# Hybrid decoder block on one core: a transpose of attention factors handed on one step later, one of two gather copies on ScalarE in the late steps, and two merge loads written in front of a loop's end

## The chip, the core and the metric

The kernel runs on one core of a Trainium2 chip. A core has TensorE (PE: matmuls, with PEld for its weight loads), VectorE (DVE), ScalarE (ACT), GpSimd (POOL) and SyncE (SP), which here issues nearly all transfers between the chip's memory and the core. Each engine works through its own instructions in the order in which they were written; engines wait for one another by semaphores. Results of matmuls go to eight banks of an accumulation memory, here two rings of four, named "mm" and "acc".

The metric is the device time of one execution in microseconds (us). The kernel before takes 1875.59 us, the median of three runs (1875.35 to 1877.91).

## The reference

One layer, 1024 tokens of width 1024, everything in float32:

```python
h = h + 0.5 * swiglu(rms_norm(h, ffn1_norm), ffn1_w1, ffn1_w3, ffn1_w2)
u = rms_norm(h, mix_norm)
proj = u @ w_in                     # q, k, v of 12 heads; 512 pooled channels; two gates
y_attn = dilated_mixture_attention(q, k, v) @ w_branch_attn
y_pool = multiscale_pool(pz, pool_w, pool_scale) @ w_branch_pool
merged = gates[:, :, 0] * y_attn + gates[:, :, 1] * y_pool
h = h + merged @ w_out
h = h + 0.5 * swiglu(rms_norm(h, ffn2_norm), ffn2_w1, ffn2_w3, ffn2_w2)
return rms_norm(h, final_norm)
```

The attention has three groups of four heads, each with its own window and dilation. Every group gives an output and a softmax denominator for each token; the three outputs of a head slot are added with weights that come from the three denominators. Those weights are called factors below.

## The kernel before

Every float32 factor of a product is split into a high and a low part, and a product is three matmuls: high by high, high by low, low by high. ACT makes the high part by a copy, DVE or POOL the low part by a subtraction. The large products are done in blocks, with sums and differences of blocks, so that seven products stand for eight.

The program goes through the first feed-forward net (0 to about 600 us), the input projection (to about 1020), the token mixers with the pooled branch (to about 1135), the merge and the output projection (to about 1236), and the second feed-forward net with the last norm.

**The first products.** `run_first(n, ks, terms)` (matmuls at line 1158) makes the first product of quad n over the blocks ks of the inner dimension. Term 0 is high by high, 1 is high by the low part of the input x, 2 is the low part of the weight by high. Quads 0 and 1 have a bank each (u_first); both need the low parts xlo_b_f of blocks 2 and 3, which DVE makes.

**The mixers.** Attention works on 48 slots: two pairs of heads (hp), three groups, eight blocks of queries. The loop takes two slots a step; q counts 24 steps. In step q, PE makes the scores s (for two steps at a time, when q is even), turns the exponentials of step q-1 (`trans_p`, tile tp), does pieces of the pooled branch's product (yp) as filling, and makes the outputs of step q-2 (`values`, tile o). ACT makes the high part of the turned exponentials (ehi), splits the next ring of queries and keys (line 1590), and takes the exponentials (e). DVE copies the outputs of step q-3 from their bank to their place by token (`gather`, two copies of 64 partitions by 256, line 2071), masks the scores and makes the low parts elo. `house(s)` does what falls due at a slot: statistics out and back, loads of values, and the next piece of the factors.

**The factors.** `make_factors(hp, eng)` is a generator; each `advance` runs it to its next `yield`. For head pair 0 it makes the factors f by small operations, turns them on PE (f_turned, line 1917, into an "mm" bank), copies them out by ACT (1919), stores them (f_by_head, 1920), and, a yield later, loads them spread over the partitions by four loads f_of (1928; two for the first half of the tokens, two for the second). For head pair 1 it spreads them by two copies of ACT and one of DVE (1937, 1935).

**Combining.** `combine(hp, half, ...)` multiplies the three outputs of a half of the tokens with their factors and adds them: for hp 0 on POOL (lines 2081 and 2085), then ACT makes the high part att (2090) and POOL the low one (2091). For hp 1, after the loop, PE turns the factors (fa), DVE multiplies (2083), and POOL and DVE add. Steps 20 to 23 take hp 0's pieces between the other work; the last piece of the second half follows after the loop, in front of the last pair's ehi on ACT.

**After the loop.** Eight pieces n of hp 1's combining alternate with the last of the 48 pieces of the pooled branch. `end_branches` multiplies a finished pooled product by its gate (line 2124), and `send` stores it (by_pool, 2134). `load_merge(k)` loads a gate and a pooled product (2161, 2162) for merge k. Then PE multiplies by the branch weights (ya), DVE and POOL merge, and the output projection wo (2368) begins with the merged sums' high and low parts (o_hi, o_lo).

Of the kernel before, what the change touches and what calls it, by code (L numbers as in the profile page):

```python
# [12 lines left out]
AF = mybir.ActivationFunctionType  # L13
# [124 lines left out]
def tile_block(  # L138
# [895 lines left out]
    def begin_up1():  # L1034
# [94 lines left out]
        banks = {}  # L1129
# [20 lines left out]
        def run_first(n, ks, terms):  # L1150
            if n not in banks:
                banks[n] = quads[n].bank["x"] = bank("mm", f"u_first{n}")
            w, (hi, lo) = first[n], X["b11"]
            for i in terms:
                for k in ks:
                    r = slice(k * P, (k + 1) * P)
                    a, b = three((w[:, 0, r], w[:, 1, r]), (hi[:, k, :], lo[:, k, :]))[i]
                    pe.matmul(banks[n], a, b, start=(k == 0 and i == 0), stop=(k == 3 and i == terms[-1]))

        FRONT, BACK = slice(0, 2 * P), slice(2 * P, HALF)  # L1160
        high("b11", 0, xt(0, 0), gain(0))
# [31 lines left out]
            high("b11", k, xt(0, k), gain(k))  # L1193
        for k in (2, 3):
            low("b11", k, xt(0, k), gain(k))
        run_first(0, (2, 3), (0, 2, 1))
        run_first(1, (2, 3), (0, 2, 1))
        operand(2, 1)
        operand(3, 1)
        high_b21(4)  # L1200
# [186 lines left out]
    class Mix:  # L1387
# [56 lines left out]
        def send(self):  # L1444
            for a in range(2):
                nc.sync.dma_start(gate_dram[self.g][:, a], self.y[a])
# [447 lines left out]
    def make_factors(hp, eng):  # L1894
# [19 lines left out]
        if hp == 0:  # L1914
            yield
            p = bank("mm", "f_turned")[:GROUPS * 2 * NT, :P]
            pe.transpose(p, by_head.rearrange("p g a i -> p (g a i)"), ident)
            turned = att_small.tile([GROUPS * 2 * NT, P], F32, name="f_turned")
            ac.activation(turned, p, AF.Copy)
            nc.sync.dma_start(f_dram.rearrange("g a i p -> (g a i) p"), turned)  # L1920
            yield
# [133 lines left out]
    def gather(q):  # L2055

        hp, g, i = slots[2 * q]
        del T[2 * q], T[2 * q + 1]
        p = outs.pop(q).rearrange("p (s a c) -> p s a c", s=2, a=2)
        if i == 0:  # L2060
            own[hp, g] = sums_o.tile([P, S], F32, tag="o", bufs=HPAIRS * GROUPS, name=f"o{hp}_{g}")
        o = own[hp, g]
        if g == 0:
            o = o[:, i * P:(i + 2) * P].rearrange("p (s c) -> p s c", s=2)
        elif g == 1:
            o = o.rearrange("p (b c r) -> p r b c", b=2, r=4)[:, i // 2]
        else:
            o = o.rearrange("p (c i) -> p i c", i=NT)[:, i:i + 2]
        for a in range(2):
            r = slice(a * HD, (a + 1) * HD)  # L2070
            ve.tensor_copy(o[r], p[r, :, a, :])

    att_parts = {}

# [115 lines left out]
    def house(s):  # L2190

        u, i = divmod(s, NT)
        if i == 1 and u > 0 and slots[s - 2][1] != 0:
            send_stats(*slots[s - 2][:2])
        if s - N // 2 in (8, 9, 10, 11, 12):
            advance(factors[0])
        if i == 4 and u + 1 < len(uses):
            load_values(uses[u + 1])
# [8 lines left out]
    with tc.manual_schedule():  # L2207
# [6 lines left out]
                    for hp, (adds, lower) in enumerate((((gp, gp), gp), ((gp, ve), ve)))]  # L2214
        splits = {}
        for q in range(N // 2):
            send()
            if q % 2 == 0:
                scores(q)
                scores(q + 1)  # L2220
            for half in {20: (0, 0), 21: (0,), 22: (0, 1), 23: (1, 1)}.get(q, ()):
                advance(combines[0][half])
            if q == 0 or q % 2 == 1:
                next(fill, None)
            if q > 0:
                trans_p(q - 1)
                splits[q - 1] = split_p(q - 1)
                next(fill, None)
                if q % 4 == 1:
                    next(fill, None)  # L2230
# [46 lines left out]
        for n in range(8):  # L2277
            advance(combines[1][n // 4])
            if n not in (3, 5, 7):
                next(fill, None)  # L2280
            end_branches()
            send()
            if n == 3:
                load_merge(2)
        for k in (3, 4):
            load_merge(k)
    assert next(fill, None) is None
    left_b.close()
    xstack.close()
# [398 lines left out]
```

## Time and profile before

| what | us |
|---|---|
| median of three runs | 1875.59 |
| the profiled execution | 1877.42 |
| its span, from the first to the last instruction | 1875.2 |
| PE busy | 1863.7 |
| DVE busy | 1366.2 |
| POOL busy | 783.9 |
| ACT busy | 768.4 |
| transfers, mean | 181 GB/s |

The granted clock of PE was 0.999 of full speed over the span. A row of the timeline gives the start and the length of one instruction, or of a few that follow one another on one engine, then engine, line, operation, out<-in, shapes, the count, and in brackets how long the engine sat idle before and what ended that. A row of groups gives total busy time and the mean length in ns. A row of stretches gives, for each engine, its busy us and instructions, then the granted clock, the share of the 16 transfer engines that were busy, and GB/s.

### The profile page before, as it was taken

What the parts mean: (1) busy time and instruction counts of PE and PEld (TensorE: products, weight loads), DVE (VectorE), ACT (ScalarE), POOL (GpSimd) and SP (SyncE); (2) the same over time, 40 slices, a digit from 0 to 9 for tenths busy, and PEclk for the clock granted to TensorE, in tenths of its full rate; (3) what the DMA queues carried; (4) which work ended last, traced back from release to release, by engine and by line L of the source; (5) the groups of instructions that cost most, each with busy time, mean ns of one, the idle gap of its engine ahead of it and who ended that gap; (6) DMA issues with size and microseconds to landing.
All of it is one profiled execution on the core that took longest, in us unless ns stands there. A gap on an engine that the chain in (4) does not pass through costs nothing.

```text
span 1875.2 us, 24419 instructions
## 1 busy us (share of the span) xinstructions
PE 1863.7 (99%) x8667; PEld 1545.1 (82%) x8667; DVE 1366.2 (73%) x1966; ACT 768.4 (41%) x1393; POOL 783.9 (42%) x569
## 2 busy tenths in 40 slices
PE   9999999999999999999999999999999999999998
PEld 8888888888888888888888887888888888888886
DVE  7887866668886776658885886887765566577867
ACT  7422323233345643334445772463333333343344
POOL 5554644452222364445554467544333333312221
PEclk9999999999999999999999999999999999999999
DMA  8134324356565436765578888634332233354654
GB/s 327 45 124 149 121 95 152 117 206 209 192 231 198 157 114 208 258 211 185 213 251 324 314 254 298 267 129 180 120 139 85 90 107 122 126 203 157 223 197 146
DMA packets 148369, 339.70 MB, mean 181 GB/s; under 512 B 18024, under 2 KB 39576, under 8 KB 146712
## 3 DMA queue, kind: packets, MB, share of 16 engines
q1 hardware_dynamic: 144504, 327.30, 50.1%
q10 hardware_dynamic: 3744, 10.85, 1.6%
q8 instruction: 68, 1.11, 0.2%
q14 instruction: 53, 0.43, 0.1%
HBM read 237.48 MB, written 100.62 MB: 180 GB/s over the span
## 4 chain that ended last, share of the span: by engine, by line
PE 55%; DVE 2%; ACT 2%; DMA 1%; issue 1%; POOL 1%; SPq 0%; ACTq 0%; POOLq 0%; DVEq 0%
PE u_mixm L334 15%; PE d_f L904 8%; PE wo L2368 4%; PE yp L2110 2%; PE o L2048 1%; PE u_f20a L334 1%; PE u_f20b L334 1%; PE u_f21b L334 1%; PE u_f21a L334 1%; PE u_f210b L334 1%; PE u_f210a L334 1%; PE u_f29b L334 1%; PE u_f29a L334 1%; PE u_f28b L334 1%; PE u_f28a L334 1%; PE u_f27b L334 1%
## 5 line engine op out<-in xcount | busy, mean ns | idle before, releaser
L904 PE MATMUL d_f<-bhi_f,ahi_f 128*128 128x512 f32 x616 | 240.2, 390 | 0.0
L904 PE MATMUL d_f<-bhi_f,alo_f 128*128 128x512 f32 x616 | 239.8, 389 | 0.0
L904 PE MATMUL d_f<-blo_f,ahi_f 128*128 128x512 f32 x616 | 239.7, 389 | 0.0
L861 POOL TENSOR_TENSOR alo_f<-g_f,ahi_f 128x512 fp32r<-128x512 f32 x60 | 86.7, 1462 | 269.0 <-ACT ahi_f L857 269.0
L334 PE MATMUL u_mixm<-xhi_t_mix,wc_mixm 128*128 128x512 f32 x608 | 157.3, 391 | 0.1
L904 PEld LDWEIGHTS d_f<-bhi_f,alo_f 128*128 128x128 f32 x616 | 115.6, 188 | 24.3 <-DVE alo_f L861 0.2
L904 PEld LDWEIGHTS d_f<-bhi_f,ahi_f 128*128 128x128 f32 x616 | 115.6, 188 | 24.1 <-ACT h L424 0.5
L904 PEld LDWEIGHTS d_f<-blo_f,ahi_f 128*128 128x128 f32 x616 | 115.7, 188 | 24.0
L334 PEld LDWEIGHTS u_mixm<-xhi_t_mix,wc_mixm 128*128 128x128 f32 x608 | 113.5, 188 | 23.8 <-ACT wc_mixm L322 0.5
L334 PE MATMUL u_mixm<-xhi_b_mix,wc_mixm 128*128 128x512 f32 x456 | 120.3, 391 | 0.0
L325 POOL TENSOR_TENSOR wc_mixm<-s_mixm,wc_mixm 128x512 fp32r<-128x512 f32 x52 | 77.1, 1483 | 101.8 <-ACT wc_mixm L322 95.7
L334 PEld LDWEIGHTS u_mixm<-xhi_b_mix,wc_mixm 128*128 128x128 f32 x456 | 84.9, 188 | 17.2
L322 ACT ACTIVATE wc_mixm<-s_mixm 128x512 fp32r<-128x512 f32 x76 | 47.0, 628 | 111.4 <-DVE s_mixm L378 56.4
L857 ACT ACTIVATE ahi_f<-g_f 128x1024 fp32r<-128x1024 f32 x84 | 81.9, 975 | 6.8 <-DMA g_f<-gs_f 6.6
L334 PE MATMUL u_mixm<-xlo_t_mix,wc_mixm 128*128 128x512 f32 x304 | 81.3, 389 | 0.0
L325 POOL TENSOR_TENSOR wc_mixm<-raw,wc_mixm 128x512 fp32r<-128x512 f32 x41 | 62.3, 1522 | 37.9 <-ACT wc_mixm L322 24.6
L2368 PE MATMUL wo<-w_o,o_hi 128*128 128x512 f32 x224 | 69.4, 391 | 0.0
L646 POOL TENSOR_TENSOR y_f<-y_f,norm_ffn 128x512 f32<-128x512 f32 x35 | 54.4, 1560 | 35.5 <-DVE y_f L627 25.2
L857 ACT ACTIVATE bhi_f<-s_f2w 128x512 fp32r<-128x512 f32 x55 | 32.9, 627 | 86.0 <-DVE s_f2w L879 69.6
L857 ACT ACTIVATE bhi_f<-s_f1w 128x512 fp32r<-128x512 f32 x55 | 33.1, 629 | 83.5 <-DVE s_f1w L879 70.8
L334 PEld LDWEIGHTS u_mixm<-xlo_t_mix,wc_mixm 128*128 128x128 f32 x304 | 57.1, 188 | 12.0
L861 DVE TENSOR_TENSOR alo_f<-g_f,ahi_f 128x1024 fp32r<-128x1024 f32 (+1 forms) x48 | 58.6, 1222 | 7.7 <-ACT ahi_f L857 7.7
(1360 smaller groups left out, 4823.4 us busy)
## 6 DMA issues: line engine op xcount, KB each, us to landing
g_f<-gs_f SPq DMA_DIRECT2D x70, 512.0 KB
gs_f<-y_f SPq DMA_DIRECT2D x88, 256.0 KB
raw<-in_w2a_dram SPq DMA_DIRECT2D x35, 512.0 KB
raw<-in_w2b_dram SPq DMA_DIRECT2D x35, 512.0 KB
gs_f<-gb_f SPq DMA_DIRECT2D x46, 256.0 KB
raw<-in_w1b_dram SPq DMA_DIRECT2D x22, 512.0 KB
raw<-in_w3b_dram SPq DMA_DIRECT2D x22, 512.0 KB
raw<-in_w1a_dram SPq DMA_DIRECT2D x20, 512.0 KB
```

The costliest lines, as they stand in the source:

```text
L322: ac.activation(w[:, 0], src, AF.Copy)
L325: eng.tensor_tensor(w[:, 1], src, w[:, 0].bitcast(F32), op=OP.subtract)
L334: pe.matmul(p, a, b, start=(start and n == 0), stop=(n == 11), skip_group_check=not start)
L646: gp.tensor_tensor(c, c, self.sv.norm[:, cols], op=OP.mult)
L857: ac.activation(hi[:, c], src, AF.Copy)
L861: eng.tensor_tensor(lo[:, d], src[:, o], hi[:, d].bitcast(F32), op=OP.subtract)
L904: pe.matmul(self.banks[m][t], l, r, start=(first and q == 0), stop=(last and q == 2))
L2048: pe.matmul(p, l, r, start=(j == 0), stop=(j == end))
L2110: pe.matmul(p, a, b, start=(j == 0), stop=(j == 11))
L2368: pe.matmul(banks[m][t], l, r, start=(st == 0 and j == 0 and q == 0), stop=(st == 1 and j == 1 and q == 2))
```

## The change

It has four parts. In the first products, the terms 0 and 2 of both quads over blocks 2 and 3 now come before term 1 of both. The turned factors get one more `yield`, and their pieces other places. From the gather of step 17 on, the second of the two copies goes from DVE to ACT; and the pieces of hp 0's combining in steps 22 and 23 change order. The loads of merges 3 and 4 are written into the loop after it.

```diff
@@ run_first
-                    pe.matmul(banks[n], a, b, start=(k == 0 and i == 0), stop=(k == 3 and i == terms[-1]))
+                    pe.matmul(banks[n], a, b, start=(k == 0 and i == 0), stop=(k == 3 and i == 1))
@@ the first products
-        run_first(0, (2, 3), (0, 2, 1))
-        run_first(1, (2, 3), (0, 2, 1))
+        for terms in ((0, 2), (1,)):
+            for n in (0, 1):
+                run_first(n, (2, 3), terms)
@@ make_factors
             pe.transpose(p, by_head.rearrange("p g a i -> p (g a i)"), ident)
+            yield
             turned = att_small.tile([GROUPS * 2 * NT, P], F32, name="f_turned")
             ac.activation(turned, p, AF.Copy)
             nc.sync.dma_start(f_dram.rearrange("g a i p -> (g a i) p"), turned)
@@ gather
         for a in range(2):
             r = slice(a * HD, (a + 1) * HD)
-            ve.tensor_copy(o[r], p[r, :, a, :])
+            if a == 1 and 3 * N // 8 - 1 <= q:
+                ac.activation(o[r], p[r, :, a, :], AF.Copy)
+            else:
+                ve.tensor_copy(o[r], p[r, :, a, :])
@@ house
-        if s - N // 2 in (8, 9, 10, 11, 12):
+        if s - N // 2 in (8, 9, 10, 12):
             advance(factors[0])
@@ the loop over q
         for q in range(N // 2):
+            if 2 * q == N // 2 + 14:
+                advance(factors[0])
             send()
...
-            for half in {20: (0, 0), 21: (0,), 22: (0, 1), 23: (1, 1)}.get(q, ()):
+            for half in {20: (0, 0), 21: (0,), 22: (1, 1), 23: (0, 1)}.get(q, ()):
                 advance(combines[0][half])
...
                 splits[q - 1] = split_p(q - 1)
+                if 2 * q == N // 2 + 12:
+                    advance(factors[0])
                 next(fill, None)
@@ after the loop
             send()
-            if n == 3:
-                load_merge(2)
-        for k in (3, 4):
-            load_merge(k)
+            if n in (3, 4, 5):
+                load_merge(n - 1)
```

N is 48, so the transpose of the factors goes from the end of step 17 to step 18, behind `trans_p`; its copy and store to the end of step 18, in front of that slot's loads of values and statistics; and the four loads f_of to the start of step 19.

On ACT, the copy of the turned factors stands here before. ehi is the high part of the turned exponentials of one step, xlo_b_mix<-xhi_b_mix the split of a ring, and e the exponentials of one slot:

```order
L1995 ACTIVATE e_9743,own_stats_2_9681<-e_9743,own_stats_2_9681 128x128 x2
L1995 ACTIVATE e_9746,own_stats_2_9681<-e_9746,own_stats_2_9681 128x128 x2
L1919 ACTIVATE f_turned<-f_turned 48x128
L2027 ACTIVATE ehi_9825<-tp_0_9801 128x512
L1590 ACTIVATE xlo_b_mix<-xhi_b_mix 128x512 x2
L1995 ACTIVATE e_9819,own_stats_2_9681<-e_9819,own_stats_2_9681 128x128 x2
L1995 ACTIVATE e_9822,own_stats_2_9681<-e_9822,own_stats_2_9681 128x128 x2
```

And now, at the same place:

```order
L1997 ACTIVATE e_9743,own_stats_2_9681<-e_9743,own_stats_2_9681 128x128 x2
L1997 ACTIVATE e_9746,own_stats_2_9681<-e_9746,own_stats_2_9681 128x128 x2
L2029 ACTIVATE ehi_9822<-tp_0_9796 128x512
L1591 ACTIVATE xlo_b_mix<-xhi_b_mix 128x512 x2
L1997 ACTIVATE e_9816,own_stats_2_9681<-e_9816,own_stats_2_9681 128x128 x2
L1997 ACTIVATE e_9819,own_stats_2_9681<-e_9819,own_stats_2_9681 128x128 x2
L1921 ACTIVATE f_turned<-f_turned 48x128
```

The copy has moved behind the whole of the next step.

On SP, the store and the loads of the factors stand here before, between loads for the pooled branch (gb, wab), values (v) and statistics (stats):

```order
L1627 DMA gb_9756<-gate_3625 128x1024
L1920 DMA f_by_head<-f_turned 48x128
L2134 DMA by_pool_8629<-gb_9247 128x1024
L1928 DMA f_of_9838<-f_by_head 64x3x512 x4
L1611 DMA v_0_in<-v_3612 128x1024
L1611 DMA v_1_in<-v_3612 128x1024
L1889 DMA stats_8617<-st_1_8622 128x8x4
L1622 DMA wab_9950<-late_w_105 128x2x512
```

And now:

```order
L1628 DMA gb_9756<-gate_3625 128x1024
L2139 DMA by_pool_8629<-gb_9247 128x1024
L1922 DMA f_by_head<-f_turned 48x128
L1612 DMA v_0_in<-v_3612 128x1024
L1612 DMA v_1_in<-v_3612 128x1024
L1890 DMA stats_8617<-st_1_8622 128x8x4
L1930 DMA f_of_9843<-f_by_head 64x3x512 x4
L1623 DMA wab_9950<-late_w_105 128x2x512
```

A pooled store has moved ahead of the factors' store, and two loads of values and one of statistics ahead of the four loads f_of.

Further on in SP's queue stand the merge loads of the loop's end, each a gate and a pooled product; by_pool_8632 is the last pooled store. Before:

```order
L2161 DMA merge_10277<-gate_3623 128x512
L2162 DMA merge_10277<-by_pool_8629 128x512
L2134 DMA by_pool_8632<-gb_9952 128x1024
L2161 DMA merge_10308<-gate_3625 128x512
L2162 DMA merge_10308<-by_pool_8631 128x512
L2161 DMA merge_10311<-gate_3620 128x512
L2162 DMA merge_10311<-by_pool_8626 128x512
```

And now:

```order
L2166 DMA merge_10277<-gate_3623 128x512
L2167 DMA merge_10277<-by_pool_8629 128x512
L2139 DMA by_pool_8632<-gb_9952 128x1024
L2166 DMA merge_10292<-gate_3625 128x512
L2167 DMA merge_10292<-by_pool_8631 128x512
L2166 DMA merge_10302<-gate_3620 128x512
L2167 DMA merge_10302<-by_pool_8626 128x512
```

In this queue nothing has moved: the pooled branch's last piece ends with n = 4, and its store is sent in front of the load that n = 4 now makes.

On POOL, the low part of hp 0's first half moves behind the first three operations of the second half; on ACT, the high part of the first half goes from step 22 to step 23, each ACT copy of a gather stands in front of that step's ehi, and the last three stand behind the spreading of hp 1's factors.

## The prediction

> **What bounds the kernel now.** I read the page's busy rows first, then TensorE's list of waits, then the timeline around each wait that the change touches.
>
> ```profile
> PE 1863.7 (99%) x8667; PEld 1545.1 (82%) x8667; DVE 1366.2 (73%) x1966; ACT 768.4 (41%) x1393; POOL 783.9 (42%) x569
> PE u_first L1158 <- DVE xlo_b_f L1066: 1.0, 1, 1.0
> PE wo L2368 <- DVE o_lo L2356: 0.7, 1, 0.7
> PE f_turned L1917 <- POOL f L1912: 0.6, 1, 0.6
> PE tp L2015 <- ACT e L1995: 0.2, 1, 0.2
> ```
>
> The first row: TensorE (PE) works 99% of the span. The others are its waits (total, times, longest). No matmul is removed, so the most that can be won is their sum, 1.0 + 0.7 + 0.6 + 0.2 = 2.5 us, of 1877.4 us. A loss has no such bound. So the question is which of these waits go, and whether a larger one opens.
>
> **Part 1, the first products (line 1158).** The second pair of quads now runs its high terms ahead of the low term that PE waited for.
>
> ```profile
> 10.38 0.39 PE L1158 MATMUL u_first<-xlo_b_f,wc_first 128*128 128x512 f32 x1
> 11.75 0.50 PE L1158 MATMUL u_first<-xlo_b_f,wc_first 128*128 128x512 f32 x1 [0.98 <-DVE xlo_b_f L1066]
> 13.49 1.09 PE L334 MATMUL u_f11a<-xhi_b_f,wc_f11a 128*128 128x512 f32 x4
> 44.09 0.60 ACT L610 ACTIVATE y_f<-u_f12a 128x512 f32<-128x512 f32 x1 [0.41 <-PE u_f12a L334]
> 57.06 2.35 PE L334 MATMUL u_f10a<-xhi_t_f,wc_f10a 128*128 128x512 f32 x8
> ```
>
> Matmuls in a row start 0.23 us apart (1.09 us for four, less the last one's 0.39, over three). Four of them, 0.91 us, now stand ahead of the one at 10.38, which so starts at 11.29; its successor starts at 11.75 as before, since VectorE's low part (xlo_b_f) is no earlier, and u_f11a starts at 12.6 instead of 13.5: 0.9 us won there. It is not all kept. At 44.09 ScalarE waited for PE only 0.41 us, so its chain, and with it VectorE's, can move up by that much; at 57.06 eight matmuls take 2.35 us where eight without a stall take 7 x 0.23 + 0.39 = 2.0, so PE is held there by that chain. I take 0.4 won, with ends 0 and 0.9.
>
> **Part 2, the turned factors.** The transpose of the head factors (f_turned) goes behind the next scores and transposes; its copy by ScalarE (ACT) and the store f_by_head go to the end of that step, the four loads f_of one step on.
>
> ```profile
> 1096.20 0.29 PE L1917 MATMUL f_turned<-ident,f 128*48 128x128 f32 x1 [0.62 <-POOL f L1912]
> 1096.43 0.33 PE L1968 MATMUL s<-qk_hi,qk_hi 64*128 64x128 f32 x2
> 1098.67 0.60 ACT L2027 ACTIVATE ehi<-tp 128x512 fp32r<-128x512 f32 x1 [1.86 <-PE tp L2015]
> 1101.65 0.19 ACT L1995 ACTIVATION_READ_ACCUMULATOR e<-e,own_stats 128x1 f32 x1
> 1096.53 0.27 ACT L1919 ACTIVATE f_turned<-f_turned 48x128 f32<-48x128 f32 x1 [1.70 <-PE f_turned L1917]
> ```
>
> The scores at 1096.43 can start when the outputs before them are through, some 0.9 us earlier (the 0.62 us wait and the transpose's own place). ACT waited for PE at 1098.67 (1.86 us), so its step moves up 0.9 us as well, and ends at 1101.84 - 0.9 = 1100.94. The transposes that waited 0.2 us for it gain too. The moved transpose needs a bank that the masks of the new scores free; no row shows that wait, so I bound it by 0 and the 0.62 us of the old one and take 0, the nearer to a step in which PE and the masks run side by side. So **0.9 us is won at this place**.
>
> But the copy now stands behind all of that step on ACT: 1100.94 + 0.27 = 1101.2, where it ended at 1096.8. The store follows at once, 4.4 us later than before. And SyncE (SP) now has two loads of values and one of statistics in front of the f_of loads:
>
> ```profile
> 1096.83 0.33 SPq L1920 DMA_DIRECT2D f_by_head<-f_turned  x1
> 1098.31 2.61 SPq L1928 DMA_DIRECT2D f_of<-f_by_head  x4
> 1100.96 1.39 SPq L1611 DMA_DIRECT2D v_in<-v  x2
> 1102.39 0.51 SPq L1889 DMA_DIRECT2D stats<-st  x1
> f_of<-f_by_head SPq DMA_DIRECT2D x4, 384.0 KB
> v_in<-v SPq DMA_DIRECT2D x2, 512.0 KB
> 1095.00:1098.00 3.00, 2.38 (x31) 1.98 (x31) 1.98 (x10) 0.27 (x1) 0.71 (x3) 1.00 0.03 8
> 1098.00:1100.00 2.00, 2.00 (x14) 1.83 (x15) 0.98 (x6) 1.33 (x3) 0.14 (x1) 1.00 0.73 284
> 1100.00:1102.00 2.00, 1.89 (x11) 1.12 (x9) 1.97 (x4) 1.84 (x9) 2.00 (x2) 1.00 0.62 173
> 1102.00:1104.00 2.00, 2.00 (x15) 1.68 (x15) 1.53 (x10) 1.74 (x4) 0.93 (x2) 1.00 1.08 266
> 1104.00:1106.00 2.00, 2.00 (x29) 1.87 (x28) 1.96 (x7) 1.44 (x8) 2.00 (x3) 1.00 1.06 214
> 1112.00:1114.00 2.00, 2.00 (x30) 1.87 (x29) 1.96 (x6) 0.63 (x1) 1.26 (x2) 1.00 1.08 411
> DMA packets 962, 0.34 MB, mean 281 GB/s; under 512 B 867, under 2 KB 867, under 8 KB 962
> ```
>
> Store at 1101.25, then 0.3 + 1.0 + 0.5 us of issues: the first f_of load is issued at about 1103.1 instead of 1098.31. The stretches (last column GB/s, the one ahead of it the DMA share) show what the queue then does. The values, 1.05 MB at up to 411 GB/s, take 2.6 us, from 1102.9 to 1105.5. The statistics are small packets: 867 of them fill the 1.2 us from 1109.7 to 1110.9 (last row), seven us after their issue at 1102.39 and behind f_of and the values, so the queue works in order; I take their 1.2 us, to 1106.7. The first two f_of loads, 0.79 MB at the 266 and 214 GB/s of the stretches in which they moved, take 3.0 to 3.7 us: they land at about **1110.2**. The lower end is an empty queue: before, 0.57 and 0.35 MB moved in the two stretches up to 1102, of which 0.52 were a pooled store; the rest of the 0.79 MB takes 1.5 us at 266 GB/s, so they were in at 1103.5, 5.2 us after the first issue. That gives 1103.1 + 5.2 = 1108.3.
>
> GpSimd (POOL) waits for just these two loads, and works off a chain that ACT waits for:
>
> ```profile
> 1105.94 2.56 POOL L2081 TENSOR_TENSOR o<-o,f_of 128x512 f32<-128x512 f32 x2
> L2081 POOL TENSOR_TENSOR o<-o,f_of 128x512 f32<-128x512 f32 x6 | 7.7, 1302 | 0.0
> L2085 POOL TENSOR_TENSOR o<-o,o 128x512 f32<-128x512 f32 x4 | 5.2, 1290 | 0.3
> L2091 POOL TENSOR_TENSOR att<-o,att 128x512 fp32r<-128x512 f32 x2 | 2.6, 1284 | 1.5 <-ACT att L2090 1.5
> 1121.06 0.63 ACT L2090 ACTIVATE att<-o 128x512 fp32r<-128x512 f32 x1
> 1124.69 2.00 ACT L1937 ACTIVATE f_of<-f 128x1024 f32<-128x1024 f32 x2 [1.89 <-DVE f L1912]
> 1128.01 0.69 DVE L2083 TENSOR_TENSOR o<-o,fa 128x512 f32<-128x512 f32 x1
> 1141.65 0.69 DVE L2178 TENSOR_TENSOR merge<-merge,ya 128x512 f32<-128x512 f32 x1 [2.08 <-DMA merge<-gate]
> ```
>
> Between its first multiplication and ACT's second copy att stand, in the new order, six multiplications, four additions and the first low part: 6 x 1.30 + 4 x 1.29 + 1.28 = 14.3 us. The new order (the second half's start ahead of the first half's end) takes out the 0.74 us that POOL waited for ACT in the middle, but not this sum. From 1110.2 it ends at 1124.5, where ACT's copy began at 1121.06: 3.4 us later. Behind that copy on ACT stand the last pair's ehi; VectorE (DVE) makes its low part and then the second head pair's factors from there; ACT spreads them (1124.69 + 2.00, which is 5.63 us after its copy's start); and DVE's first product with them (1128.01) opens the chain to the last pooled store, the merge loads behind it, and PE's wait at wo. PE has a few pooled products between to cover it, but they are the same as before and only shift; I count the chain in full.
>
> **Part 3, seven of the gather's copies on ACT.**
>
> ```profile
> L2071 DVE COPY o<-o 64x256 f32<-64x256 f32 x16 | 8.6, 537 | 0.8 <-PE o L2048 0.7
> L2027 ACT ACTIVATE ehi<-tp 128x256 fp32r<-128x256 f32 x3 | 1.1, 377 | 1.2 <-PE tp L2015 1.2
> L2027 ACT ACTIVATE ehi<-tp 128x512 fp32r<-128x512 f32 x13 | 7.4, 596 | 5.1 <-PE tp L2015 4.9
> ```
>
> DVE loses 7 x 0.54 = 3.8 us. On ACT no such copy is in the trace; the nearest row is 0.38 us for 256 columns from the same memory, with ends 0.27 (f_turned's) and 0.60 (512 columns). Four stand in steps in which ACT waits for PE (4.9 us over 13 steps) and cost nothing; without that cover, 0.38 us each. In the last steps PE waits for neither, so DVE's relief buys nothing there either. Three come after the spread factors, on the chain above: 5.63 + 3 x 0.38 = 6.77 us from ACT's copy to DVE's product, where it was 1128.01 - 1121.06 = 6.95: 0.2 won, with ends 0.5 won and 0.5 lost.
>
> **Part 4, the merge loads.** In SyncE's order nothing moves: both loads stand behind the last pooled store as before, and DVE's 2.08 us at 1141.65 stay. I take 0. Had they moved, the 0.7 us at wo would be the most to win; their buffers, asked for earlier, could cost a wait that no row here shows, and since the queue is the same I take none.
>
> **The sum.** The late chain ends at 1110.2 + 14.3 + 6.8 = 1131.3 instead of 1128.01: +3.3 us, and the 0.9 us of part 2 are swallowed by it, since they move PE towards a wait. Less 0.4 from part 1: **+2.9 us**. The profiled execution took 1877.42 us for a span of 1875.2, and would take 1880.3; the median of the runs is 1875.59, 1.8 lower, so I forecast 1875.6 + 2.9 = **1878.5**. With the loads landed between 1108.3 and 1111.2 (each us later costs one) and part 1 between 0.9 and 0: +0.5 to +4.3, or 1876.1 to 1879.9.
>
> **The rivals.**
>
> *The factors come in time.* If f_of lands before 1106.9, POOL's chain is not late (1106.9 + 21.1 = 1128.0). Then 0.9 + 0.4 + 0.2 = 1.5 us are won: 1874.1, or 1873.3 by the better ends of parts 1 and 3. For it: 1.1 us of POOL's waits go, and the stretch 1095-1098 shows the queue nearly empty. Against it: the copy cannot come before its step on ACT ends, and 1.8 us of issues and 1 MB stand between.
>
> *The loads land together.* If the four f_of loads, all in flight at once, share the engines instead of following one another, the first two land with the last: 1.57 MB at 214 to 240 GB/s from 1106.7, at 1113.5. Then +6.6 - 0.4 = +6.2: 1881.8, **slower**. It decides from a landing at 1111.1 on, where the loss passes 3.75 us. The statistics' place in the queue speaks against it. The Trainium skill, "DMA: Bandwidth & Descriptors", section "Queues, rings and completion order", states that each DMA engine takes a ring's descriptors in ring order, though a later one may finish its write first; by that rule the sum stays with 1110.2, and by shared engines it would be the 1113.5. The trace agrees as far as the statistics go.
>
> *The clock drops.* PE's new stalls together are at most the 3.4 us by which ACT is late. If PE then ran at half its clock for as long as it had stood, 1.7 us more are lost: 1880.2. In the stretches on both sides of the 0.62 us wait the granted clock (the 1.00 ahead of the DMA share) is full, and no long wait is to be seen in this trace. The Trainium skill, "TensorE: Matmul & The Clock Gate", "What's actually happening", gives such a drop after an idle window of about 3.4 us; by that rule one stall of the whole 3.4 us would just do it, two shorter ones would not.
>
> **How the numbers follow.** Forecast 0.56, factors in time 0.26, landing together 0.12, clock 0.03, anything else 0.03. Two parts in a thousand (3.75 us: below 1871.8, above 1879.3) is about what a measurement of this kernel can tell from no change. Slower than that: 0.12 + 0.03 and the forecast's upper end, 0.08, together 0.23. Faster: 0.03, since the waits that can go sum up to less. The range runs from the first rival's lower end, 1873.3, to 1880.4, past the forecast's own and the clock's.
>
> **What would show it.** POOL's row o<-o,f_of near 1110 with a DMA as its releaser (right), or at 1105 without one (the first rival), or at 1113 (the second). ACT's att, which followed at once, with an idle time of some 3 us and POOL as releaser. A new wait of PE at o or fa near 1125. The wait at u_first gone but for 0.2 us, f_turned's 0.6 gone, wo's 0.7 still there. Wrong throughout would be a PE list of waits that is shorter by 1.5 us with nothing new in it.

## The result, and the profile after

The changed kernel takes 1880.55 us (median of 12 runs, 1879.30 to 1882.80), the kernel before, beside it, 1876.61 (12 runs, 1875.35 to 1878.65). The ratio is 1.0021 (95% interval 1.0012 to 1.0030): **3.9 us slower**, with an interval of some 1.7 us on either side. The profiled execution took 1880.64 us for a span of 1878.9.

The busy row of the changed kernel's page, to set beside that of before:

```profile
PE 1864.3 (99%) x8667; PEld 1545.0 (82%) x8667; DVE 1360.9 (72%) x1959; ACT 771.3 (41%) x1400; POOL 784.9 (42%) x569
```

TensorE does the same 8667 matmuls in the same time. Seven instructions have gone from DVE to ACT, DVE is 5.3 us less busy, and the kernel is slower all the same: the time has gone into waits. TensorE's list of waits in the changed kernel (total, times, longest):

```profile
PE o L2050 <- ACT o L2074: 1.4, 1, 1.4
PE fa L1948 <- ACT f_of L1939: 1.2, 1, 1.2
PE idle L1041 <- DVE fours L1042: 1.1, 1, 1.1
PE o L2050 <- ACT ehi L2029: 1.0, 1, 1.0
PE wo L2375 <- DVE o_lo L2363: 0.7, 1, 0.7
PE o L2050 <- DVE elo L2032: 0.7, 2, 0.3
PE tp L2017 <- ACT e L1997: 0.2, 1, 0.2
```

The 1.0 at u_first and the 0.6 at f_turned are gone. In their place stand four rows at o and fa with 4.3 us, of which 0.3 at o for DVE stood in the kernel before too; the new 4.0 lie within thirteen microseconds. wo keeps its 0.7. The timeline around them, in order of time:

```profile
1085.61 0.33 PE L1970 MATMUL s<-qk_hi,qk_hi 64*128 64x128 f32 x2
...
1099.44 0.25 ACT L1921 ACTIVATE f_turned<-f_turned 48x128 f32<-48x128 f32 x1
...
1101.52 2.75 SPq L1930 DMA_DIRECT2D f_of<-f_by_head  x4
...
1110.62 2.54 POOL L2086 TENSOR_TENSOR o<-o,f_of 128x512 f32<-128x512 f32 x2 [6.94 <-DMA f_of<-f_by_head]
...
1117.19 0.63 ACT L2095 ACTIVATE att<-o 128x512 fp32r<-128x512 f32 x1 [2.33 <-POOL o L2090]
1117.84 0.38 ACT L2074 ACTIVATE o<-o 64x256 f32<-64x256 f32 x1
1118.28 0.38 PE L2050 MATMUL o<-ehi,v_in 128*128 128x256 f32 x1 [1.38 <-ACT o L2074]
...
1123.56 1.35 POOL L2090 TENSOR_TENSOR o<-o,o 128x512 f32<-128x512 f32 x1
1124.94 0.63 ACT L2095 ACTIVATE att<-o 128x512 fp32r<-128x512 f32 x1 [3.65 <-POOL o L2090]
1128.55 2.00 ACT L1939 ACTIVATE f_of<-f 128x1024 f32<-128x1024 f32 x2 [1.88 <-DVE f L1913]
1130.99 0.69 DVE L2088 TENSOR_TENSOR o<-o,fa 128x512 f32<-128x512 f32 x1 [0.70 <-ACT o L2074]
```

Read it from the fourth row: POOL sits idle 6.94 us for the factors. ACT waits 2.33 us for POOL at the first att. Behind att on ACT stands one of the new gather copies, and PE cannot write its next outputs until that copy has emptied their bank: this is the 1.4 us at 1118.28. The second att waits 3.65 us; the ehi behind it, DVE's elo that is made from it, and the spread f_of make PE's other new waits.

To set these times beside those of before, I take a row that stands ahead of everything that part 2 moves, the first scores of the step at 1086. In the kernel before it reads

```profile
1086.94 0.33 PE L1968 MATMUL s<-qk_hi,qk_hi 64*128 64x128 f32 x2
```

so the changed kernel's execution is 1.33 us earlier there, and 1.33 has to be added to its times.

### The profile page after: what moved, and what is told of

It reads as the page before. It is cut to its first block, busy times and chain, and to the rows that moved or that the text cites. A ratio compares the mean times of both kernels' runs of the same rounds, so it can differ in the third digit from the quotient of the medians.

```text
span 1878.9 us, 24416 instructions
## 1 busy us (share of the span) xinstructions
PE 1864.3 (99%) x8667; PEld 1545.0 (82%) x8667; DVE 1360.9 (72%) x1959; ACT 771.3 (41%) x1400; POOL 784.9 (42%) x569
## 4 chain that ended last, share of the span: by engine, by line
PE 53%; DVE 2%; ACT 2%; DMA 2%; issue 1%; POOL 1%; SPq 0%; ACTq 0%; POOLq 0%; DVEq 0%
PE u_mixm L334 15%; PE d_f L904 8%; PE wo L2375 4%; PE u_f20a L334 1%; PE u_f20b L334 1%; PE u_f21b L334 1%; PE u_f21a L334 1%; PE u_f210b L334 1%; PE u_f210a L334 1%; PE u_f29b L334 1%; PE u_f29a L334 1%; PE u_f28b L334 1%; PE u_f28a L334 1%; PE u_f27b L334 1%; PE u_f27a L334 1%; PE u_f26b L334 1%
```

## The experiments

Each was timed against the kernel before on the same chip: 1876.47, 1876.54 and 1876.32 us in the three groups.

### One part alone

Four kernels, each the kernel before with one part of the diff that is printed above. Part 1, the first products:

```diff
-        run_first(0, (2, 3), (0, 2, 1))
-        run_first(1, (2, 3), (0, 2, 1))
+        for terms in ((0, 2), (1,)):
+            for n in (0, 1):
+                run_first(n, (2, 3), terms)
```

> The kernel before with part 1 alone (the pair's high terms ahead of the low ones). Step 1 as predicted: 0.4 us won, with ends 0 and 0.9, and TensorE's start stall near 57 us grows by what is lost of the 0.9. Rival, read off the changed kernel's trace, where the stalls that both kernels have stand 1.35 us earlier at 1022 us: the whole is kept and more, 1.3 us won, and the stall near 57 us stays as it is.

Measured: 1876.45 us, ratio 1.0001 (0.9992 to 1.0010). Neither number is seen in the time. The traces say why the 1.3 us were a misreading: TensorE's start in the changed kernel, and in a kernel without part 1 (part 2 alone, below).

```profile
6.56 0.71 PE L1158 MATMUL u_first<-xhi_b_f,wc_first 128*128 128x512 f32 x2
...
12.17 1.07 PE L334 MATMUL u_f11a<-xhi_b_f,wc_f11a 128*128 128x512 f32 x4
```

```profile
6.83 0.73 PE L1158 MATMUL u_first<-xhi_b_f,wc_first 128*128 128x512 f32 x2 [1.00 <-ACT wc_first L1144]
...
12.69 0.62 PE L334 MATMUL u_f11a<-xhi_b_f,wc_f11a 128*128 128x512 f32 x2
```

From the first product to u_f11a it takes 5.61 us with part 1 and 5.86 without. Over all kernels of this study it is 5.61 to 6.38 us with the part (nine profiles, the middle one 5.68), and 5.86 to 6.08 without it, but for the profile of before, which had 6.87 (five, the middle one 6.06). The 1.0 us at u_first belonged to that execution, in which the low parts came late: DVE's two subtractions ahead of the wait took 3.0 us there (8.68 to 11.69), and 1.7 to 1.9 in the other four kernels without the part. In the second fence TensorE waits 1.0 us as well, but for the high parts of the weights, ahead of everything. The middle profiles are 0.4 us apart, but the two groups overlap (part 1 alone itself took 6.38), so no gain of part 1 is shown. The 1.35 us by which the changed kernel's trace was early at 1022 us are there nearly whole at u_f11a (12.17 against 13.49): they are for the most part the late low parts of the one execution.

Part 2, the factors:

```diff
+            yield                          # behind the transpose f_turned
-        if s - N // 2 in (8, 9, 10, 11, 12):
+        if s - N // 2 in (8, 9, 10, 12):
+            if 2 * q == N // 2 + 14:
+                advance(factors[0])
+                if 2 * q == N // 2 + 12:
+                    advance(factors[0])
-22: (0, 1), 23: (1, 1)
+22: (1, 1), 23: (0, 1)
```

> The kernel before with part 2 alone (transpose, copy, store and loads of the factors moved, and the new order of the combines). Theory: the late factors carry the whole loss; the changed kernel is 3.9 us slower and part 1 wins 0.4 to 1.3, so this one is 4.3 to 5.2 us slower than before, with GpSimd's first product at about 1112 and its wait for a DMA. Rival: the copies on ScalarE carry a share, because TensorE's first new wait in the changed kernel is for an output bank that such a copy reads; then this one loses 3.3 us or less.

Measured: 1881.56 us, ratio 1.0030 (1.0018 to 1.0041), **5.1 us slower**. The theory holds: this part alone costs as much as the whole change, by the medians 1 us more. Its timeline has the same chain, without a copy in it:

```profile
1110.96 2.54 POOL L2082 TENSOR_TENSOR o<-o,f_of 128x512 f32<-128x512 f32 x2 [6.73 <-DMA f_of<-f_by_head]
...
1117.52 0.63 ACT L2091 ACTIVATE att<-o 128x512 fp32r<-128x512 f32 x1 [2.11 <-POOL o L2086]
1119.66 1.90 PE L2016 MATMUL tp<-ident,e 128*128 128x128 f32 x8 [0.81 <-ACT e L1996]
...
1125.27 0.63 ACT L2091 ACTIVATE att<-o 128x512 fp32r<-128x512 f32 x1 [4.19 <-POOL o L2086]
1126.44 0.39 PE L2049 MATMUL o<-ehi,v_in 128*128 128x256 f32 x1 [1.58 <-ACT ehi L2028]
...
1132.20 0.69 DVE L2084 TENSOR_TENSOR o<-o,fa 128x512 f32<-128x512 f32 x1
```

Where the changed kernel's first wait was at o, for a copy's bank, TensorE here waits at its transposes, for the exponentials. Both stand behind the first att on ACT. Which of them TensorE waits for is not the cause; that ACT stands still for POOL is.

Part 3, the copies:

```diff
-            ve.tensor_copy(o[r], p[r, :, a, :])
+            if a == 1 and 3 * N // 8 - 1 <= q:
+                ac.activation(o[r], p[r, :, a, :], AF.Copy)
+            else:
+                ve.tensor_copy(o[r], p[r, :, a, :])
```

> The kernel before with part 3 alone (seven gather copies on ScalarE). Theory: within 0.3 us of before, as no copy stands behind a wait of ScalarE for GpSimd. Rival: a copy holds an output bank while ScalarE waits for GpSimd in att, also where the factors are in time: TensorE waits some 1.4 us at its outputs and the kernel is 0.5 to 1.4 us slower.

Measured: 1874.93 us, ratio 0.9992 (0.9983 to 1.0001). Better than the theory: some 1.5 us faster, with no change just inside the interval. The rival is out: where the factors come in time, TensorE's list has no wait at o for a copy on ACT.

Part 4, the merge loads:

```diff
-            if n == 3:
-                load_merge(2)
-        for k in (3, 4):
-            load_merge(k)
+            if n in (3, 4, 5):
+                load_merge(n - 1)
```

> The kernel before with part 4 alone (the loop's load_merge calls). Theory: the queue of SyncE is the same, 0.0 us, and TensorE's 0.7 us at wo stays. Rival: the loads come earlier in some way and wo's wait shrinks, 0.7 us faster.

Measured: 1877.11 us, ratio 1.0003 (0.9994 to 1.0012): no difference that can be seen, as the unchanged queue of SyncE says.

### The changed kernel without one part

Without part 3 (all gather copies on DVE again):

```diff
-            if a == 1 and 3 * N // 8 - 1 <= q:
-                ac.activation(o[r], p[r, :, a, :], AF.Copy)
-            else:
-                ve.tensor_copy(o[r], p[r, :, a, :])
+            ve.tensor_copy(o[r], p[r, :, a, :])
```

> The changed kernel without part 3 (all gather copies on VectorE). Theory: the factors alone cost 5.1 us and the copies win about 0.9 of it at VectorE's first product (1130.99 - 1124.94 = 6.05 us behind ScalarE's att, where it was 6.95): 1881.5, and TensorE's wait at o for a copy's bank is replaced by one of the same length elsewhere. Rival: the copies behind att cost TensorE 1.4 us at o: 1879.1.

Measured: 1881.50 us, ratio 1.0026 (1.0016 to 1.0037), the theory's number, with an interval of 2 us on either side. By the medians the copies win about 1 us (1881.50 against 1880.55) also where one of them is seen to hold up TensorE; the intervals of the two overlap.

Without part 2 (the diff of part 2 above, reversed; parts 1, 3 and 4 stay):

> The changed kernel without part 2 (parts 1, 3 and 4 alone). Theory: part 2 carries all of the loss, so this one is 0.5 to 1.8 us faster than before (1874.8 to 1876.0): what the copies win, and a little of part 1. Rival: parts 1, 3 and 4 together cost something that they don't cost apart; then it is slower than before.

Measured: 1874.81 us, ratio 0.9993 (0.9984 to 1.0002). All of the loss is gone, and the rest of the change is by the medians some 1.5 us faster than before, with no change just inside the interval. In TensorE's list of waits nothing stands at o for ACT, and nothing at fa (d_f lies far from the mixers):

```profile
PE idle L1041 <- DVE fours L1042: 1.0, 1, 1.0
PE f_turned L1918 <- POOL f L1913: 0.6, 1, 0.6
PE d_f L904 <- POOL alo_f L861: 0.6, 1, 0.6
PE o L2049 <- DVE elo L2031: 0.3, 1, 0.3
```

### How late may the factors be?

Four kernels change the landing of f_of, or what follows it, by other means. In the first, the loads go ahead of the values and the statistics:

```diff
         if s - N // 2 in (8, 9, 10, 12):
-            advance(factors[0])
+            advance(factors[0], 2 if s - N // 2 == 12 else 1)
...
-            if 2 * q == N // 2 + 14:
-                advance(factors[0])
```

> The changed kernel with the four f_of loads right behind the store, ahead of the values and the statistics. Theory: what is late is the landing of f_of, and each us of it costs one. The loads no longer wait for 1 MB of values and 1024 packets of statistics, only some 1.5 us for the store, and their first half lands 2 to 3 us earlier than GpSimd's first product at 1110.6: 2 to 3 us of the 3.9 lost come back, 1877.6 to 1878.6. Rival: the loss comes from the order on ScalarE and TensorE (transpose, copies, combines), not from the landing: no change from the changed kernel, 1880.5.

Measured: 1878.99 us, ratio 1.0011 (1.0002 to 1.0020). 1.6 us of the 3.9 come back by the medians, less than the 2 to 3 of the theory; the rival's no change is not what came. The landing moved by 2.2 us (1108.92 here, and the scores' row is 0.49 us later than in the changed kernel); and something had to be given for it:

```profile
1108.92 2.54 POOL L2086 TENSOR_TENSOR o<-o,f_of 128x512 f32<-128x512 f32 x2 [4.76 <-DMA f_of<-f_by_head]
```

```profile
1115.32 0.50 PE L2050 MATMUL o<-ehi,v_in 128*128 128x256 f32 x2 [1.15 <-DMA v_in<-v]
```

The values that now stand behind f_of in the queue are late for TensorE, 1.15 us. So are the statistics of the second head pair for DVE, as the table below takes up.

The second is the kernel before with the moved transpose, but the copy right behind that step's ehi, and the loads at their old place in the queue (of its edit, the lines that part 2 doesn't have):

```diff
             if q > 0:
                 advance(splits[q - 1], 2)
+                if 2 * q == N // 2 + 12:
+                    advance(factors[0])
```

> The kernel before with the transpose moved as in the change, but its copy on ScalarE right behind that step's ehi (ahead of the exponents), and store and loads in their old places in the queue. Theory: the 0.95 us that TensorE wins by the moved transpose stays, since the loads are only 1.8 us later, against 3.8 in the change; GpSimd's first product near 1106 to 1106.7 on the clock of the profile of before, and 0 to 0.95 us faster than before. Rival: any delay of the store makes GpSimd late, 1 us slower.

Measured: 1878.50 us, ratio 1.0011 (1.0003 to 1.0020), 2.0 us slower. The theory failed: even this small delay is more than POOL has to spare. It starts at 1106.89 plus 1.26 us between the scores' rows, 1108.15 on the clock of before, 2.2 us later than there. In this kernel the two halves are in their old order, so the first att comes earlier in ACT's program and stands idle longer, and TensorE's transposes, which wait for the exponentials behind it, are drawn out:

```profile
1113.46 0.63 ACT L2091 ACTIVATE att<-o 128x512 fp32r<-128x512 f32 x1 [3.67 <-POOL o L2086]
...
1115.61 1.91 PE L2016 MATMUL tp<-ident,e 128*128 128x128 f32 x8 [0.24 <-ACT e L1996]
```

In the kernel before the same eight transposes take 1.04 us:

```profile
1117.24 1.04 PE L2015 MATMUL tp<-ident,e 128*128 128x128 f32 x8
```

The list of waits shows only the 0.24 us in front of the first of the eight; the rest of this stall, 0.87 us, lies between the pairs and counts as busy. In the changed kernel, too, eight transposes are drawn out so, to 1.91 us at 1119.87.

The third is the changed kernel (all four parts) with the same early copy:

> The changed kernel with the copy right behind ehi and the loads ahead of the values, as in the last kernel. Theory: the whole loss goes and what parts 2 and 3 win is left, 0.4 to 1.8 us faster than before (1874.7 to 1876.1). Rival: copies and combines carry a cost of their own, which would be left: slower than before by over 1 us.

Measured: 1877.66 us, ratio 1.0007 (0.9999 to 1.0016). 2.9 of the 3.9 us come back; not the whole, so the theory's number was missed. GpSimd's first product is again 2 us late, though its chain is shorter: from there to the second att it takes 15.1 us in early copy, in the old order of the combines, and 14.3 here, in the new one.

A fourth takes a piece out of GpSimd's chain in that kernel, and leaves the landing where it is (the line that is new):

```diff
+        combines[0][0] = combine(0, 0, (gp, gp), ve)
```

> The kernel with the early copy and all four parts (1877.7), with the first half's low part taken out of GpSimd's chain (1.28 us) and given to VectorE. Theory: ScalarE's second att is late by GpSimd's chain, so it comes 1.2 us earlier, and the kernel takes 1876.5. Rival: VectorE's masks wait behind the low part, for ScalarE's first att, and what is won there is lost at the scores: 1877.7 or slower.

Measured: 1876.81 us, ratio 1.0003 (0.9994 to 1.0011). That is 0.9 us less than without it, or 0.6 when each is set against the kernel before in its own group, where the theory had 1.2; the intervals overlap. The second att is 0.9 us earlier.

```profile
1119.28 1.85 PE L2017 MATMUL tp<-ident,e 128*128 128x128 f32 x8
...
1120.63 0.63 ACT L2095 ACTIVATE att<-o 128x512 fp32r<-128x512 f32 x1
```

Set side by side, the kernels give the price of being late. "Second att" is its start, counted from the scores' row of the same trace (in the kernel before 1121.06 - 1086.94 = 34.12 us) and less those 34.12; "DVE's product" is the same for DVE's first product o<-o,fa (in the kernel before 1128.01 - 1086.94 = 41.07); "cost" is the median less that of the kernel before in the same group.

| kernel | second att late by, us | DVE's product late by, us | cost, us |
|---|---|---|---|
| copies on DVE: part 1 alone | 0.0 | 0.0 | 0.0 |
| part 4 alone | 0.0 | 0.0 | +0.6 |
| early copy | 2.2 | 2.2 | +2.0 |
| the change without part 3 | 4.9 | 4.9 | +5.0 |
| part 2 alone | 5.0 | 5.0 | +5.1 |
| copies on ACT: part 3 alone | 0.0 | -0.9 | -1.5 |
| the change without part 2 | 0.0 | -0.9 | -1.5 |
| the same with the merges early (below) | 0.0 | -0.9 | -1.6 |
| early copy, low part on DVE | 0.3 | 0.5 | +0.5 |
| the change with early copy | 1.2 | 1.2 | +1.1 |
| the change with loads first | 3.0 | 3.1 | +2.5 |
| the change | 5.2 | 4.3 | +3.9 |
| the change with half the loads later (below) | 7.0 | 6.1 | +5.7 |

With the copies on DVE each microsecond of the second att costs one. With them on ACT five kernels lie 1.3 to 1.6 us below that line, and three do not: their product comes 6.9 to 7.1 us behind att, not 6.05. There another load is late, the statistics of the second head pair, from which DVE makes that pair's factors. The early copy with the low part on DVE, and for comparison the change without part 2:

```profile
1122.38 0.29 DVE L1904 TENSOR_TENSOR top<-top,stats 128x16 f32<-128x16 f32 x1 [1.75 <-DMA stats<-st]
```

```profile
1120.95 0.18 DVE L1904 TENSOR_TENSOR top<-top,stats 128x16 f32<-128x16 f32 x1 [0.20 <-DMA stats<-st]
```

In the other two of the three DVE waits 2.07 and 3.38 us there, and one of the small operations behind takes 1.19 and 1.27 us, where it takes 0.2 in the change without part 2. In the changed kernel DVE waits 1.47 us for the statistics, but then 2.33 more for the ehi behind att, so that they don't count. By DVE's product all thirteen kernels lie on one line: what a kernel costs is what this product is late by, within 0.8 us.

### What the landing is made of

POOL needs two of the four f_of loads. Stretches of the changed kernel (last column GB/s):

```profile
1101.00:1104.50 3.50, 3.50 (x37) 3.06 (x36) 2.18 (x11) 3.45 (x13) 2.54 (x2) 1.00 0.79 273
1104.50:1106.00 1.50, 1.50 (x11) 1.36 (x10) 1.50 (x3) 1.50 (x8) 0.00 (x0) 1.00 1.15 196
1106.00:1108.00 2.00, 2.00 (x14) 1.70 (x13) 2.00 (x11) 1.81 (x6) 0.00 (x0) 1.00 0.83 199
1108.00:1110.00 2.00, 2.00 (x18) 1.73 (x18) 1.76 (x3) 1.85 (x8) 0.00 (x0) 1.00 1.07 229
```

By the trace's packets the statistics were through at 1105.5. From there, 0.1 MB up to 1106, 0.4 to 1108 and the rest at 229 GB/s make the 0.79 MB of two loads at 1109.3 (the 384th of their 2 KB packets ended at 1109.05); POOL started 1.3 us after that. One run asked what these 1.3 us are, by taking the other two loads out of the way:

```diff
             for c in (LOWS, HIGHS):
+                if c is HIGHS:
+                    yield
...
-        if s - N // 2 in (8, 9, 10, 12):
+        if s - N // 2 in (8, 9, 10, 12, 16):
```

> The changed kernel with two of the four f_of loads (the left half of the columns, all that GpSimd's first product needs) at their place and the other two behind the next wab and gb loads. In the profiles so far GpSimd starts 1.3 to 1.6 us after the 384th of the 768 packets of f_of has ended. Theory: that is what a transfer takes from its last packet to the engine that waits, so it stays 1.2 to 1.6, and the time stays at 1880.5. Rival: the four loads share the engines and the first two end with a part of the last two; then the 1.3 to 1.6 fall below 0.7, and the kernel is 0.7 us faster or more.

Measured (5 runs): 1881.97 us, ratio 1.0028 (1.0016 to 1.0040). POOL's first product was no earlier, and the other half now is late as well:

```profile
1111.72 2.54 POOL L2088 TENSOR_TENSOR o<-o,f_of 128x512 f32<-128x512 f32 x2 [7.26 <-DMA f_of<-f_by_head]
...
1119.74 2.54 POOL L2088 TENSOR_TENSOR o<-o,f_of 128x512 f32<-128x512 f32 x2 [1.52 <-DMA f_of<-f_by_head]
```

The 384th packet of 2 KB had ended at 1109.80, 1.9 us ahead of the first row: neither the 1.2 to 1.6 nor the 0.7. The wab load that took the place of the two loads has packets of the same size, and ran behind the first two as they had, so the time of this run alone settles nothing.

The traces do. They also hold the moments at which each load's semaphore, on which the waiting engine waits, was raised: sixteen times a load. In the changed kernel the sixteen of the second f_of load come from 1109.25 to 1110.49, and POOL starts at 1110.62; in the run with half the loads they come from 1109.31 to 1111.59, and POOL starts at 1111.72. In all eight kernels in which POOL waits for these loads it starts 0.13 us after the last of the sixteen. Ahead of the raises stand sixteen packets of 4 bytes, which in the changed kernel end from 1108.35 to 1109.55. So the 1.3 us there are 0.25 from the estimate of 1109.3 to the last of these packets, 0.94 from it to the last raise, and 0.13 to POOL's start. The four loads land one behind the other, with their last raises at 1108.69, 1110.49, 1112.28 and 1114.19. In the run with half the loads the sixteen are spread over 2.3 us instead of 1.2, which goes with its longer 1.9 us.

### The merge loads, moved for good

The change without part 2, with the loads called two rounds earlier, so that they stand in front of the last pooled store:

```diff
-            if n in (3, 4, 5):
-                load_merge(n - 1)
+            if n in (1, 2, 3):
+                load_merge(n + 1)
```

> The last kernel with load_merge called two rounds of the loop earlier, so that both loads really stand in front of the last pooled store in SyncE's order. Theory: TensorE's stall at wo, which was 0 to 0.9 us in the profiles so far, is gone, and the kernel is about 0.4 us faster than the last one. Rival: the store behind them comes later and the stall only moves, no change.

Measured: 1874.70 us, ratio 0.9991 (0.9982 to 1.0000), 0.1 us from the kernel without the edit (1874.81): the 0.4 us of the theory are not there. The profile has no wait at wo, but neither had that of the kernel without the edit, so it doesn't show whether the wait moved or was not to be had. How much the waits there change is seen at DVE's fourth merge. It waits 2.08 us in the kernel before, 0.75 with part 1 alone and 1.23 with part 4 alone, three kernels with the same order of SyncE. In the changed kernel, and in the kernel with part 3 alone:

```profile
1144.92 0.69 DVE L2183 TENSOR_TENSOR merge<-merge,ya 128x512 f32<-128x512 f32 x1 [2.25 <-DMA merge<-gate]
```

```profile
1138.61 0.69 DVE L2181 TENSOR_TENSOR merge<-merge,ya 128x512 f32<-128x512 f32 x1 [0.31 <-DMA merge<-gate]
```

These two kernels, the change without part 2 with and without the edit (1874.7 and 1874.8 us), have the lowest medians of all, with part 3 alone (1874.9) beside them. Against the kernel before, the upper end of the interval is at no change.

## Why the prediction was right and wrong

The forecast was +2.9 us, through one mechanism: factors that land late, GpSimd's chain behind them, ScalarE's att, and TensorE behind that. The mechanism is the one that cost the time; +3.9 was measured. Term by term, with 1.33 us added to the changed kernel's times:

| step | forecast | measured |
|---|---|---|
| ACT's copy of f_turned ends | 1101.2 | 1101.0 |
| first f_of load issued | 1103.1 | 1102.85 |
| bytes of the first two f_of through | 1110.2 | 1110.6 |
| **first two f_of landed (POOL's first product)** | 1110.2 | **1111.95** |
| POOL's chain to the second att | 14.3 us | 14.3 us (1110.62 to 1124.91) |
| second att to DVE's first product | 6.8 us | 6.05 us (1124.94 to 1130.99) |
| DVE's first product | 1131.3 | 1132.3 |
| the chain, against 1128.01 | +3.3 | +4.3 |
| part 1 | -0.4 | -0.4 between the middle profiles, not shown in the time |

That +4.3 and -0.4 give just the 3.9 is in part luck: behind the scores' row the two profiled executions differ by 5.0 us (793.3 and 788.3 us to the end), and part 1's share is not clear of its spread.

**The step that failed is the landing, mis-sized by 1.75 us.** The first product was to be at the end of the statistics, 1106.7, plus 0.79 MB at 214 to 266 GB/s, 3.0 to 3.7 us. The start of that sum is right (1105.5 + 1.33 = 1106.8) and the rate is nearly so (196 to 229 GB/s); together they account for 0.4. The other 1.3 us are a term that the sum put at nothing: the two loads were taken to land as soon as their bytes could have been moved. What the runs show in its place is that POOL starts 0.13 us behind the last of the load's sixteen raises, and that this one came 0.94 us behind the last of the 4-byte packets. The same term was in the trace of before: the prediction had the two loads in at 1103.5 there, the 384th packet ended at 1103.61, and the last raise came at 1105.50. The Trainium skill, "DMA: Bandwidth & Descriptors", section "Why a DMA increments its semaphore by 16 and not by 1", says that the engines of one transfer finish independently and that the waiter needs them all. The trace agrees, with sixteen raises spread over 1.24 us and POOL behind the last.

The rival in which all four loads land together (1113.5) is out: their last raises stand 1.8 to 1.9 us apart, in the order of the queue. That the landing lies half way between forecast and rival is chance.

The step from the store to the first load was right in part by luck. The sum took 1.0 us for the issue of the two loads of values, where its own row has 1.39; here it took 0.89.

**The upper bound of the landing was too low.** It was put at 1111.2 us without a working (the slowest rate of the sum gives 1106.7 + 3.7 = 1110.4), and the range ended at 1880.4 us, 0.15 us below what came. The rest of the miss in the absolute time is the level: the forecast stood on a median of three runs, 1875.59, where twelve gave 1876.61.

**The copies on ACT** were put at 0.2 us. The medians give 1.0 to 1.5, which the intervals do not part from nothing; the traces give 0.9 at DVE's first product. The mean copy costs ACT more than the 0.38 us assumed:

```profile
L2074 ACT ACTIVATE o<-o 64x256 f32<-64x256 f32 x7 | 3.3, 496 | 0.6 <-DVE o L2076 0.5
```

The first three take 0.65 to 0.67 us each, the fourth 0.38, and the three behind the loop 0.92 together, so on the chain the 0.38 was no error. What was missed is DVE's side: it was said that its relief buys nothing in the last steps. DVE's row ahead of its first product in the kernel with part 2 alone, and in the changed one:

```profile
1129.54 2.62 DVE L2072 COPY o<-o 64x256 f32<-64x256 f32 x6
```

```profile
1129.21 1.07 DVE L2076 COPY o<-o 64x256 f32<-64x256 f32 x3
```

Six gather copies stood on the chain, 2.62 us, and three are left, 1.07 us. DVE then waits 0.70 us for the last one on ACT, and its product follows att by 6.05 us instead of 6.93. The sum had counted ACT's three copies there and not DVE's.

**One step was missing.** The sum counted the second att alone. The first att, too, holds ACT (2.33 us), and with it the exponentials, the gather copy and TensorE. That it adds little to the end, since TensorE would have waited for the second att otherwise, is argued from the table and not tried by itself; but TensorE's first new wait was at 1118 and not near 1125.

**Right for the stated reason:** f_turned's 0.6 us gone, SyncE's order unchanged by part 4, and the factors not in time. wo's 0.7 us is still there too, but that wait is 0.2 us with part 4 alone and not in the list with part 1 alone, where the order is the same. Nor did the clock drop; the stretches of the changed kernel in which TensorE has its new waits have a granted clock of 1.00 (the third number from the end):

```profile
1116.00:1118.30 2.30, 0.92 (x5) 0.40 (x3) 0.00 (x0) 1.06 (x3) 2.30 (x2) 1.00 1.03 379
...
1124.00:1127.00 3.00, 1.62 (x8) 0.90 (x7) 0.92 (x2) 1.73 (x4) 2.18 (x2) 1.00 0.96 318
1127.00:1130.00 3.00, 1.75 (x14) 1.55 (x15) 2.77 (x10) 1.45 (x2) 0.00 (x0) 1.00 0.75 296
```

The decision point of the rival in which they come in time, 1106.9, agrees with the experiments: in the change with early copy POOL's first product is at 1108.0 on the clock of before and the second att 1.2 us late, so it would have been in time from 1106.8. That is for the new order of the combines. In the old one there is next to nothing to spare: in the kernel before the last raise came at 1105.50, and POOL, busy up to its start at 1105.94, began 0.3 us later than the landing would have let it.

**Part 1** was given a size that the time can't show, and the row it was argued from, 1.0 us at u_first, was no property of the kernel: of five profiles without the part, one shows it.

What stays open: why the raises come 0.9 us behind the packets, and why the sixteen are spread over 1.2 us in one run and 2.3 in another; what the new order of the combines is worth by itself in the time, which was not tried; and the up to 0.8 us between a kernel's cost and the delay of DVE's product.

## What to carry to other kernels

Before a producer is moved back to fill a gap of 0.6 us on the busiest engine, follow its result to the last consumer and count what has to spare there: here the landing had 0.3 us to spare and GpSimd none, and nearly each microsecond beyond came back at the end. Follow the other loads of the queue to their consumers too: in three kernels the statistics, and no longer att, were what held DVE's product. When a landing is estimated, bytes over bandwidth is its lower end; the waiter needs the last raise of the semaphore, which in these kernels came 1.1 to 1.9 us behind the 384th packet. And a wait in a single profile (u_first, wo) should be looked for in a second execution before it is counted as something to win.

## What was not expected of the hardware

Waits move by a microsecond between executions of kernels with the same code there: TensorE's way from the first product to u_f11a took 5.86 to 6.87 us in five kernels without part 1, where two subtractions on DVE took 1.7 to 3.0 us, and DVE's wait at the fourth merge was 0.75, 1.23 and 2.08 us in three kernels with the same order on SyncE. An ACT copy of 64x256 elements takes 0.65 us in the first three of the seven and 0.38 in the fourth; in the kernel the first three write every eighth element of their target, the others in one piece. DVE's own copies differ in the same way (0.65 and 0.42 us). No run separates this from their place in the program.
